# Gate and up projections of a feed-forward stage by seven block products instead of eight

## The chip, the core and the metric

The kernel runs on one core of a Trainium2 chip. The core has a matrix engine (TensorE, PE in the profile; its weight loads are listed as PEld), a vector engine (VectorE, DVE), a scalar engine (ScalarE, ACT), a general engine (GpSimd, POOL) and a queue that issues transfers (SyncE, SP). Matrix products are accumulated in eight banks of PSUM, each 2 KB for each of 128 partitions; DVE and ACT read them from there. All other operands lie in SBUF. The metric is the device time of one execution in microseconds (us).

## The reference

Two layers of a transformer-like trunk over 512 tokens of width 1024, all in float32: three token mixers merged by gates, an output projection, a feed-forward stage, and a gated input embedding. The change concerns the feed-forward stage (`D_FF` is 2816) and touches the output projection ahead of it:

```python
merged = (ga * (ya @ w_br_a[i]) + gb * (yb @ w_br_b[i])
          + gc * (yc @ w_br_c[i]))
x = x + merged @ w_o[i]
h = rmsnorm(x, norm_ffn[i])
x = x + (jax.nn.silu(h @ w_ffn_gate[i]) * (h @ w_ffn_up[i])) @ w_ffn_down[i]
h = rmsnorm(x, norm_ple[i])
x = x + jax.nn.sigmoid(h @ w_ple_gate[i]) * (p[i] @ w_ple_in[i])
```

where `rmsnorm(x, g)` is `x / sqrt(mean(x * x) + eps) * g` over the width.

## The kernel before

Activations lie transposed: a tile has 128 channels on the partitions and the 512 tokens along the free dimension, so `x` is eight tiles of 128x512. Weights are stored on the host in blocks: a block holds all input channels for 128 output channels, as 128 partitions x (k, 128).

**Products in three terms.** To keep float32 accuracy with the faster 32-bit matmul type (float32r), each operand is split into a rounded high half and the rest (`split`, L160 to L162: ACT copies the high half, L141, and DVE subtracts it from the source, L155). A product is three matmuls: high weight by high activation (L175), high by low (L176), low by high (L177). `gemm` (L179) makes one output block of 128x512 from up to eight k-blocks for each load of weights, 8 x 3 = 24 matmuls. Every matmul has its own weight load.

**Weights.** `weights` (L164) takes a raw buffer (tag `wr`), issues one transfer into it on SP's queue (L169), and splits it into `wh` and `wl`. Each of these three tags has three buffers of 128x1024. These instructions get a priority 400 places ahead of their place in the program, so that they run as early as the buffers allow.

**Order.** The order of TensorE's instructions is the order of the program (it is kept by hand). The order on the other engines is made by a scheduler at build time from the priorities and from when operands and buffers are free; on the chip each engine then works through its queue strictly in that order. Buffers of one tag are handed out as earlier tiles of the tag are released. A count of matmul groups (`chunk`, `tick`) paces side work such as the norms, which are generators that go on after so many ticks.

**The norm.** The scale of a token, `1 / sqrt(...)`, isn't known when the products of the norm's output begin. So the projections run on `x * g`, and the scale, spread over the partitions (`self.rb`), is multiplied in afterwards; what needs it is put off by `ready` until it is there. `sumsq` squares on ACT and adds up on DVE; `norm` turns the sums with PE, takes the power on POOL and turns the result back.

**Output projection, `w_o` (L859).** For each of eight blocks m: 24 matmuls, the sum with the old `x` on DVE, then `norm_chunk`: the two halves of `x * g` as a tile `h` and the square.

**Feed-forward, `ffn` (L881).** For each of two halves: 11 blocks f, each with one gate and one up product over the eight `h` (both 128x512, in banks of tag `mm`), the gate's scale, Silu, scale, product with up, and a split into `md`; then eight down blocks over the 11 `md` of this half, each added to `x` straight from its bank. The very first gate and up blocks go through `pair` (L192), which runs two output blocks over all but the last k, then the last k of both, so that the last `h` can be late. In the second half each finished `x` goes through `norm_chunk` for the next norm.

**Banks.** Eight: three of tag `mm`, two `sc`, two `tr`, one `av`. The feed-forward stage uses `mm`, and `tr` for turning the norm's sums.

A part that has matmuls of 256 columns already is `values` (L555 and on): two outputs of 128x256 share one bank, and each matmul there (L571, L573, L575) has its own weight load too.

Of the kernel before, what the change touches and what calls it, by code (L numbers as in the profile page):

```python
# [12 lines left out]
F32R = mybir.dt.float32r  # L13
I32 = mybir.dt.int32
AF = mybir.ActivationFunctionType
ALU = mybir.AluOpType
# [4 lines left out]
P = 128  # L21
L = 2
# [3 lines left out]
D = 1024  # L26
# [13 lines left out]
HB = NFB // 2  # L40
# [19 lines left out]
class Net:  # L60
# [228 lines left out]
    def build(self):  # L289
        nc, tc, a = self.nc, self.tc, self.a  # L290
        self.bufs = dict(wr=3, wh=3, wl=3, h=8, qk=2, kh=2, v=4, pt=2, y=5, z=5, x=4, t=7, rp=4,
# [15 lines left out]
    def opening(self):  # L307
# [10 lines left out]
        for _ in range(WARM):  # L318
# [5 lines left out]
                "rp": [self.sb("rp", [P, 384]) for _ in range(4)],  # L324
# [86 lines left out]
    def layer(self, i, h, xsrc, xs):  # L411
# [43 lines left out]
        h = self.ffn(h, x)  # L455
        return self.ple(h, x, xs, self.inputs())
# [302 lines left out]
    def diff_in(self, head, st, ys):  # L759
# [99 lines left out]
    def w_o(self, mg, xsrc):  # L859
        self.phase = "wo"  # L860
        xs, h, st = [], [], []
        for m in range(KD):
# [16 lines left out]
        return xs, h  # L879

    def ffn(self, h, x):  # L881
        self.phase = "ffn"
        i = self.i
        st, hn = [], []
        for half in range(2):
            mids = []
            for f in range(HB):
                fb = half * HB + f
                g = self.sb("t", [P, 512])
                md = self.sb((["z"] * 5 + ["y"] * 5 + ["pt"])[f], [P, 2, 512], F32R)  # L890
                mids.append(md)
                pg, pu = self.ps("mm"), self.ps("mm")
                if fb == 0:
                    self.pair((pg, pu), (self.a["w_fg"][i, fb], self.a["w_fu"][i, fb]), h)
                else:
                    self.gemm(pg, self.a["w_fg"][i, fb], h)

                def gate(pg=pg, g=g):
                    self.tt(g, pg, self.rb, ALU.mult)
                    self.act(g, g, AF.Silu, table="silu")  # L900
                    self.tt(g, g, self.rb, ALU.mult)

                self.ready(gate)
                if fb:
                    self.gemm(pu, self.a["w_fu"][i, fb], h)

                def up(pu=pu, g=g, md=md):
                    self.tt(g, g, pu, ALU.mult)
                    self.split(md[:, 0, :], md[:, 1, :], g)

                self.ready(up)
            for m in range(KD):
                ps = self.ps("mm")
                self.gemm(ps, self.a["w_fd"][i, half, m], mids)
                self.tt(x[m], x[m], ps, ALU.add)
                if half:
# [257 lines left out]
def _layout(v):  # L1174
# [4 lines left out]
    for i in range(L):  # L1179
# [6 lines left out]
    down = f["w_ffn_down"].reshape(L, 2, HB * P, D)  # L1186
# [14 lines left out]
        "w_fg": _blocks(f["w_ffn_gate"]),  # L1201
        "w_fu": _blocks(f["w_ffn_up"]),
        "w_fd": _blocks(down),
# [18 lines left out]
```

## Time and profile before

| | |
|---|---|
| median of 3 runs | 1824.58 us |
| lowest, highest | 1824.06, 1826.75 us |
| span of the profiled execution (no other time of it is given) | 1827.5 us |
| first layer: matmuls of gate and up, first half | 506.7 to 627.15 us |
| first layer: down blocks of the first half | 627.4 to about 687 us |
| second layer: first matmul of gate and up to the last down blocks | from about 1440 to 1768 us |
| 512 KB blocks of weights in the feed-forward stages | 44 gate, 44 up, 32 down (and 32 of 192 KB) |
| transfers issued by POOL | none |

The span is cut into 40 slices in the page's second part, a digit for the busy tenths of each. An engine's busy time alone says little for PE, since its matmuls overlap and their ends are modelled: for PE the distance between the starts of successive matmuls is what can be read. For the other engines, a row that names an idle time before it and a releaser says what the instruction waited for.

### The profile page before, as it was taken

Reading aid. Unit: us, or ns where it says so; the run is one execution under the profiler, and the core shown is the slowest. Engines: PE = TensorE matmul, PEld = TensorE weight load, DVE = VectorE, ACT = ScalarE, POOL = GpSimd, SP = SyncE. Lnnn points to the kernel's source line nnn. Section 1 sums busy time; section 2 is a strip of 40 time slices with the busy share of each in tenths; the row PEclk is TensorE's granted clock in tenths of the full one; section 3 lists DMA queues with packets and bytes.
Section 4 is the critical chain, followed back from the end, with each engine's and each line's share of the span. In section 5 each row is a group of like instructions: output and inputs, shape, how many; then the busy total and the mean of one; then the engine's idle time right before and its main releaser. Section 6 shows DMA issues by size and latency. Waiting matters only on the chain.

```text
span 1827.5 us, 23665 instructions
## 1 busy us (share of the span) xinstructions
PE 1815.3 (99%) x8820; PEld 1527.3 (84%) x8820; DVE 1191.9 (65%) x1928; ACT 763.5 (42%) x1325; POOL 24.4 (1%) x58
## 2 busy tenths in 40 slices
PE   9999999999999999999999999999999999999998
PEld 7888888888888888888888888888888888888887
DVE  7788887887654434445777878878885444344456
ACT  5476555225432222323545755452353322232334
POOL 0000000000000000000000000000000000000000
PEclk9999999999999999999999999999999999999999
DMA  5565541325423233223436655323263232322232
GB/s 199 154 195 168 147 130 45 110 96 163 151 93 103 77 110 104 93 77 108 167 121 189 188 158 153 99 70 96 97 209 106 93 104 77 116 95 93 84 112 93
DMA packets 90881, 221.13 MB, mean 121 GB/s; under 512 B 12176, under 2 KB 21776, under 8 KB 90768
## 3 DMA queue, kind: packets, MB, share of 16 engines
q1 hardware_dynamic: 89616, 218.09, 38.2%
q8 instruction: 70, 1.15, 0.3%
q10 hardware_dynamic: 1152, 1.55, 0.3%
q14 instruction: 43, 0.35, 0.1%
HBM read 180.79 MB, written 7.34 MB: 103 GB/s over the span
## 4 chain that ended last, share of the span: by engine, by line
PE 96%; DVE 2%; ACT 1%; issue 1%; DMA 0%; SPq 0%; DVEq 0%; POOLq 0%; ACTq 0%
PE ffn_mm L175 13%; PE ffn_mm L177 13%; PE ffn_mm L176 13%; PE mergea_mm L175 2%; PE mergea_mm L177 2%; PE mergea_mm L176 2%; PE diff_sc L757 2%; PE gatec_mm L175 2%; PE gatec_mm L176 2%; PE gatec_mm L177 2%; PE gateb_mm L176 2%; PE gateb_mm L175 2%; PE gateb_mm L177 2%; PE wo_mm L176 2%; PE wo_mm L175 2%; PE wo_mm L177 2%
## 5 line engine op out<-in xcount | busy, mean ns | idle before, releaser
L141 ACT ACTIVATE ffn_wh<-ffn_wr 128x1024 fp32r<-128x1024 f32 (+1 forms) x152 | 144.3, 951 | 513.3 <-issue 382.8
L175 PE MATMUL ffn_mm<-wo_h,ffn_wh 128*128 128x512 f32 x704 | 274.2, 390 | 0.0
L177 PE MATMUL ffn_mm<-wo_h,ffn_wl 128*128 128x512 f32 x704 | 273.9, 389 | 0.0
L176 PE MATMUL ffn_mm<-wo_h,ffn_wh 128*128 128x512 f32 x704 | 273.9, 389 | 0.0
L155 DVE TENSOR_TENSOR ffn_wl<-ffn_wr,ffn_wh 128x1024 fp32r<-128x1024 f32 (+1 forms) x152 | 164.8, 1085 | 130.4 <-ACT ffn_wh L141 130.4
L158 DVE SCALAR_TENSOR_TENSOR conv_z<-glu_z,pre_par,conv_z 128x512 f32<-128x512 f32 x240 | 179.3, 747 | 2.9
L177 PEld LDWEIGHTS ffn_mm<-wo_h,ffn_wl 128*128 128x128 f32 x704 | 132.2, 188 | 27.5
L176 PEld LDWEIGHTS ffn_mm<-wo_h,ffn_wh 128*128 128x128 f32 x704 | 132.2, 188 | 27.3
L175 PEld LDWEIGHTS ffn_mm<-wo_h,ffn_wh 128*128 128x128 f32 x704 | 132.2, 188 | 27.3
L155 DVE TENSOR_TENSOR ffn_t<-ffn_t,ffn_mm 128x512 f32<-128x512 f32 x44 | 30.3, 688 | 114.8 <-PE ffn_mm L177 114.7
L155 DVE TENSOR_TENSOR ffn_t<-ffn_mm,wo_r 128x512 f32<-128x512 f32 x44 | 30.4, 692 | 109.7 <-PE ffn_mm L177 109.7
L141 ACT ACTIVATE mergea_wh<-mergea_wr 128x1024 fp32r<-128x1024 f32 (+1 forms) x32 | 27.1, 848 | 96.8 <-PE mergea_mm L176 70.8
L175 PE MATMUL ffn_mm<-ffn_z,ffn_wh 128*128 128x512 f32 x160 | 62.2, 389 | 0.0
L176 PE MATMUL ffn_mm<-ffn_z,ffn_wh 128*128 128x512 f32 x160 | 62.2, 389 | 0.0
L177 PE MATMUL ffn_mm<-ffn_z,ffn_wl 128*128 128x512 f32 x160 | 62.2, 389 | 0.0
L175 PE MATMUL ffn_mm<-ffn_y,ffn_wh 128*128 128x512 f32 x160 | 62.2, 389 | 0.0
L176 PE MATMUL ffn_mm<-ffn_y,ffn_wh 128*128 128x512 f32 x160 | 62.2, 389 | 0.0
L177 PE MATMUL ffn_mm<-ffn_y,ffn_wl 128*128 128x512 f32 x160 | 62.2, 389 | 0.0
L141 ACT ACTIVATE diff_a<-diff_sc,diff_s 128x512 f32<-128x512 f32 x32 | 22.0, 687 | 60.6 <-DVE diff_s L848 60.6
L848 DVE TENSOR_REDUCE diff_s<-diff_sc 128x1 f32<-128x512 f32 x64 | 42.0, 684 | 3.1 <-PE diff_sc L757 3.0
L155 DVE TENSOR_TENSOR wo_x<-wo_x,ffn_mm 128x512 f32<-128x512 f32 x32 | 22.0, 688 | 31.4 <-PE ffn_mm L177 31.4
L141 ACT ACTIVATE natten_wh<-natten_wr 128x1024 fp32r<-128x1024 f32 x24 | 25.4, 1059 | 39.7 <-issue 17.7
(608 smaller groups left out, 4644.3 us busy)
## 6 DMA issues: line engine op xcount, KB each, us to landing
ffn_wr<-w_fg SPq DMA_DIRECT2D x44, 512.0 KB, 3.2
ffn_wr<-w_fu SPq DMA_DIRECT2D x44, 512.0 KB, 3.3
ffn_wr<-w_fd SPq DMA_DIRECT2D x32, 512.0 KB, 3.5
natten_wr<-w_in SPq DMA_DIRECT2D x16, 512.0 KB, 4.2
natten_b<-bias SPq DMA_DIRECT2D x32, 256.0 KB, 2.9
diff_wr<-w_in SPq DMA_DIRECT2D x16, 512.0 KB, 3.5
gatec_wr<-w_in SPq DMA_DIRECT2D x16, 512.0 KB, 3.7
gateb_wr<-w_in SPq DMA_DIRECT2D x16, 512.0 KB, 3.5
```

What stands on the lines that cost most here:

```text
L141: i = self.nc.scalar.activation(out, in_, func, **kw)
L155: return self.nc.vector.tensor_tensor(out, a, b, op)
L158: return self.nc.vector.scalar_tensor_tensor(out, a, s, b, op0, op1)
L175: mm(out, wh, ah, start=first, stop=False)
L176: mm(out, wh, al, start=False, stop=False)
L177: mm(out, wl, ah, start=False, stop=last)
L757: self.nc.tensor.matmul(out, st4[:, u, qs], st[:, ks], start=n == 0, stop=n == 1)
L848: nc.vector.tensor_reduce(out=m[:, u:u + 1], in_=sc, op=ALU.max, axis=AX.X, negate=True)
```

## The change

The gate and up products of two neighbouring output blocks are computed as a 2x2 block product with seven multiplications instead of eight (the Strassen form in Winograd's variant, with shared sums). The 2x2 blocks are: two output blocks of 128 channels, two halves of the input channels (even and odd k-blocks), two halves of the tokens (0 to 255 and 256 to 511). Gate and up are carried side by side in the two halves of a bank.

- `w_o` no longer makes `h`. Instead, after each even block, `halves_in` scales the two token halves and forms one difference; after each odd block, `halves_out` forms the other three sums and splits the seven 128x256 operands into high and low (a split of four blocks and one of three).
- `gate_up(step)` makes two output blocks: `seven` loads and sums the weights, `product` runs 4 k-pairs x 2 (gate, up) x 3 matmuls of 128x256. Banks x (`sc`), y (`tr`) and z (`av`) hold sums that go on: x takes products 0, 2, 4 and 6 one after the other, z products 3 and 5, and the partial sums are read out between them (`c11`, `c12`, `c22`, `c21`).
- Of the four weight sums two (`s2`, `s4`) are made by DVE; the other two (`w[1,0] + w[1,1]` and `w[1,0] + w[0,0]`) by a second transfer, issued by POOL, that adds to what the first one brought. The `wr`, `wh` and `wl` tags keep three buffers; `rp` now has two of 128x1024.
- `mid` forms `silu(gate * scale) * up`; the second scale moves behind the down product, where each down block is multiplied by it before it is added to `x`.
- The down projection is done in three parts after 4, 8 and 11 steps (8, 8 and 6 blocks), each begun by a `pair`. `pair` now leaves the last two k to the end in place of one, everywhere.
- The tiles of `p` (`pairs`) are loaded once in a layer in place of twice.

```diff
@@ pair
-        ws = [self.weights(ap, 1024) for ap in aps]
         n = len(acts)
-        for ks in (range(n - 1), (n - 1,)):
+        ws = [self.weights(ap, n * P) for ap in aps]
+        for ks in (range(n - 2), range(n - 2, n)):
@@ layer
-        h = self.ffn(h, x)
-        return self.ple(h, x, xs, self.inputs())
+        h = self.ffn(h, x, pairs)
+        return self.ple(h, x, xs, pairs)
@@ diff_in
-            raw, rot = self.sb("rp", [P, 512]), self.sb("rp", [P, 512])
+            raw, rot = self.parts_of("rp", [512], 2)
@@ w_o
-            h.append(self.norm_chunk(m, xo, self.par(self.i, "ffn", m), "h", st))
+            if m == KD - 1:
+                self.sumsq(m, xo, st)
+            if m % 2 == 0:
+                ts[m // 2] = self.halves_in(m // 2, xo)
+            else:
+                self.halves_out(ts[m // 2], xo)
+            if m < KD - 1:
+                self.sumsq(m, xo, st)
+    def halves_in(self, kp, x):
...
+        self.act(raw[0], x[:, 0:256], AF.Copy, scale=g)
+        self.act(other, x[:, 256:], AF.Copy, scale=g)
+        self.tt(raw[3], raw[0], other, ALU.subtract)
+    def halves_out(self, t, x):
...
+        self.act(raw[1], x[:, 0:256], AF.Copy, scale=g)
+        self.act(raw[6], x[:, 256:], AF.Copy, scale=g)
+        self.stt(raw[2], raw[3], -1.0, raw[6], ALU.mult, ALU.subtract)
+        self.tt(raw[4], raw[6], t["other"], ALU.subtract)
+        self.stt(raw[5], raw[2], -1.0, raw[1], ALU.mult, ALU.subtract)
+        for (h, a, z), (l, _, _), b in zip(t["hi"], t["lo"], t["bases"]):
+            self.split(h, l, b[:, 0:z - a])
+    def seven(self, step):
+        nc, w = self.nc, self.a["w_gu"][self.i, step]
+        def load(src, plus=None):
+            r = self.sb("wr", [P, 1024])
+            nc.sync.dma_start(r, src)
+            if plus is not None:
+                nc.gpsimd.dma_start(r, plus, accum_op=ALU.add)
+            return r
+        def add(a, b):
+            r = self.sb("rp", [P, 1024])
+            self.tt(r, a, b, ALU.add)
+            return r
...
+        with self.tc.high_priority(offset=min(self.w_ahead, self.tc.cur_priority - self.p0)):
+            s1 = load(w[1, 0], w[1, 1])
+            a11 = load(w[0, 0])
+            s2 = add(s1, a11)
+            o11 = parted(a11)
+            a12 = load(w[0, 1])
+            s4 = add(s2, a12)
+            o12 = parted(a12)
+            if step:
+                o2, o1 = parted(s2), parted(s1)
+            else:
+                o1, o2 = parted(s1), parted(s2)
+            return [o11, o12, o2, o1, parted(load(w[1, 0], w[0, 0])), parted(s4),
+                    parted(load(w[1, 1]))]
+    def product(self, bank, op, ts, j, kps, first):
+        mm = self.nc.tensor.matmul
+        hi, lo = op
+        for kp in kps:
+            th, tl = ts[kp][j]
+            for u in range(2):
+                begin = first and kp == 0 and u == 0
+                for n, (w, t) in enumerate(((hi, th), (hi, tl), (lo, th))):
+                    mm(bank[:, u], w[:, u, kp], t, start=begin and n == 0, stop=False,
+                       skip_group_check=True)
+            self.chunk()
+    def gate_up(self, step, ts):
...
+        x, y, z = [self.ps(tag, (P, 2, 256)) for tag in ("sc", "tr", "av")]
...
+        if step == 0:
+            for bank, n, j in ((x, 0, 0), (y, 1, 1), (z, 3, 3)):
+                run(bank, n, j, range(KP - 1), True)
+        end = range(KP - 1, KP) if step == 0 else range(KP)
+        run(x, 0, 0, end, step > 0)
+        self.act(c11, x, AF.Copy)
+        run(y, 1, 1, end, step > 0)
+        self.tt(c11, c11, y, ALU.add)
+        if step == 0:
+            run(z, 3, 3, end)
+        run(x, 2, 2)
+        self.act(c12, x, AF.Copy)
+        if step:
+            run(z, 3, 3, first=True)
+        self.act(c22, z, AF.Copy, scale=-1.0)
+        run(x, 4, 4)
+        self.tt(c22, c22, x, ALU.subtract)
+        run(z, 5, 6)
+        self.tt(c12, c12, z, ALU.add)
+        first = self.mid(2 * step, g[0])
+        run(x, 6, 5)
+        self.act(c21, x, AF.Copy, scale=-1.0)
+        return [first, self.mid(2 * step + 1, g[1])]
+    def mid(self, f, g):
...
+            self.tt(gate, gate, self.rb, ALU.mult)
+            self.act(gate, gate, AF.Silu, table="silu")
+            self.tt(gate, gate, up, ALU.mult)
+            self.split(md[:, 0, :], md[:, 1, :], gate)
@@ ffn
+        for p, (first, end) in enumerate(PARTS):
             mids = []
+            for n in range(first, end):
+                mids += self.gate_up(n, ts)
+            both = [self.ps("mm") for _ in range(2)]
+            self.pair(both, self.a[f"w_fd{p}"][i, 0:2], mids)
+            for m in range(KD):
+                if m < 2:
+                    ps = both[m]
                 else:
+                    ps = self.ps("mm")
+                    self.gemm(ps, self.a[f"w_fd{p}"][i, m], mids)
+                d = self.sb("t", [P, 512])
+                self.tt(d, ps, self.rb, ALU.mult)
+                self.tt(x[m], x[m], d, ALU.add)
```

`PARTS` is `((0, 4), (4, 8), (8, 11))` and `KP` is 4. On the host the gate and up weights are laid out by step, output block, input half and k-pair, with gate and up side by side.

More of the change, by code (lines that the diff above doesn't have):

```diff
@@ L39 @@
 NFB = DFF // P
-HB = NFB // 2
+STEPS = NFB // 2
+PARTS = ((0, 4), (4, 8), (8, 11))
+KP = KD // 2
 EPS = 1e-6
@@ L884, in ffn @@
         st, hn = [], []
-        for half in range(2):
+        for p, (first, end) in enumerate(PARTS):
             mids = []
[L887 to L894, printed above, removed]
-                else:
[L896 to L916, printed above, removed]
+            for n in range(first, end):
[5 more added lines that the diff above has]
+                    ps = both[m]
+                else:
+                    ps = self.ps("mm")
[3 more added lines that the diff above has]
+                self.tt(x[m], x[m], d, ALU.add)
+                if p == len(PARTS) - 1:
                     if m in (0, 2):
```

53 lines of the change are left out of this document (44 added, 9 removed).

## The prediction

> **What bounds the kernel now.** I read the page first, then windows and the timeline of the first layer's gate and up stretch, then the waits of SP's queue. Columns of a group: count, busy us, mean ns of one, idle time before it; columns of the timeline: start us, duration us, engine, line, operation.
>
> ```profile
> span 1827.5 us, 23665 instructions
> PE 1815.3 (99%) x8820; PEld 1527.3 (84%) x8820; DVE 1191.9 (65%) x1928; ACT 763.5 (42%) x1325; POOL 24.4 (1%) x58
> PE   9999999999999999999999999999999999999998
> DVE  7788887887654434445777878878885444344456
> PEclk9999999999999999999999999999999999999999
> PE 96%; DVE 2%; ACT 1%; issue 1%; DMA 0%; SPq 0%; DVEq 0%; POOLq 0%; ACTq 0%
> L175 PE MATMUL ffn_mm<-wo_h,ffn_wh 128*128 128x512 f32 x704 | 274.2, 390 | 0.0
> 540.00:600.00 60.00, 60.00 (x267) 49.69 (x266) 27.68 (x33) 17.43 (x22) 0.00 (x0) 1.00 0.29 98
> ```
>
> PE is never idle in the stretch of the change, its clock is granted in full (1.00), and 96% of the chain that ends last is PE. In the 60 us window the columns after the length are PE, weight loads, DVE, ACT, POOL, clock, DMA share and GB/s: DVE is busy 46%, ACT 29%, the transfers 29%. So only the number and the pitch of matmuls counts, as long as DVE, ACT and the weights keep up.
>
> The 390 ns of a matmul overlap with the next one's; what sets the end is the pitch from start to start.
>
> ```profile
> 620.57 0.39 PE L175 MATMUL ffn_mm<-wo_h,ffn_wh 128*128 128x512 f32 x1
> 626.01 0.39 PE L175 MATMUL ffn_mm<-wo_h,ffn_wh 128*128 128x512 f32 x1
> ...
> 160.20 0.28 PE L571 MATMUL diff_mm<-diff_wh,glu_h 128*128 128x256 f32 x1
> 162.96 0.28 PE L575 MATMUL diff_mm<-diff_wh,glu_h 128*128 128x256 f32 x1
> 157.22 0.28 PE L571 MATMUL diff_mm<-diff_wh,glu_h 128*128 128x256 f32 x1
> 159.60 0.28 PE L575 MATMUL diff_mm<-diff_wh,glu_h 128*128 128x256 f32 x1
> ```
>
> Between the first two rows lie 24 matmuls, one 128x512 block of eight k by three: 5.44 us, 226.7 ns each. The value projections already run 128x256 with a weight load ahead of each: 24 starts in 2.76 us (23 steps, 120.0 ns) and 21 in 2.38 us (20 steps, 119.0 ns). I take 119.7. Half the width thus costs 53% of the time, not 50%.
>
> **The change: the matmuls.** Before, 2 layers x 22 blocks x 2 (gate, up) x 24 = 2112 matmuls of 512 columns: 2112 x 0.2267 = 478.8 us. After, 22 steps (11 a layer), each seven products of 4 k-pairs x 2 (gate, up) x 3 = 24 matmuls of 256: 3696 x 0.1197 = 442.4 us, 20.1 us a step and 2.87 us a product. The difference is -36.4 us, with the two measured pitches as bounds -39.0 to -35.3. An eighth of 478.8 would be 59.9; the worse pitch takes 23.5 of it back. The Trainium skill (TensorE: Matmul & The Clock Gate, Back-to-back issue gap) gives N / 2.4 + 2.5 ns for a single warm matmul, that is 215.8 and 109.2 ns here, by which the term would be an estimate of -52 us. [...]
>
> The down projection has the same 1056 matmuls of 512 in three parts as in two; its weights come in 24 loads a layer in place of 32. Nothing on PE.
>
> **DVE and ACT per step.** Durations:
>
> ```profile
> 572.99 1.06 ACT L141 ACTIVATE ffn_wh<-ffn_wr 128x1024 fp32r<-128x1024 f32 x1 [3.85 <-issue]
> 573.96 0.62 ACT L141 ACTIVATE ffn_y<-ffn_t 128x512 fp32r<-128x512 f32 x1
> 574.09 1.23 DVE L155 TENSOR_TENSOR ffn_wl<-ffn_wr,ffn_wh 128x1024 fp32r<-128x1024 f32 x1 [0.23 <-ACT ffn_wh L141]
> 575.23 0.68 DVE L155 TENSOR_TENSOR ffn_y<-ffn_t,ffn_y 128x512 fp32r<-128x512 f32 x1
> 578.61 0.69 DVE L155 TENSOR_TENSOR ffn_t<-ffn_mm,wo_r 128x512 f32<-128x512 f32 x1 [2.69 <-PE ffn_mm L177]
> ```
>
> DVE: seven low halves and two weight sums (s2, s4) at 1.23, three bank reads and six operations of the two mids at 0.69: 11.1 + 6.2 = 17.3 us of 20.1, 86% against 46% now. ACT: seven high halves at 1.06, four bank copies and four operations of the mids at 0.62: 12.4 us, 62%. Neither is the bound by its sum. By deadlines: three buffers of each weight half let the split of operand j start when product j-3 ends, 5.74 us ahead of its use, and it needs 1.06 + 0.23 + 1.23 = 2.5 us, so 3.2 us of delay are covered (today 8.4). A bank that is read and then added to again (x after products 0, 2 and 4, z after 3) has one other product, 2.87 us, between; the read needs 0.2 + 0.69:
>
> ```profile
> 627.14 0.39 PE L177 MATMUL ffn_mm<-wo_h,ffn_wl 128*128 128x512 f32 x1
> 627.57 0.69 DVE L155 TENSOR_TENSOR ffn_t<-ffn_t,ffn_mm 128x512 f32<-128x512 f32 x1 [3.36 <-PE ffn_mm L177]
> ```
>
> (0.43 us from the last matmul's start to the reader, 0.2 past its slot.) So 2 us are spare, which one 1.23 operation ahead of it in DVE's queue fits and two don't. Queued behind a late reader is PE itself. Bounds per step: 0 if every read and split falls in its window, 1.0 if one bank read a step stands behind two wide operations (0.2 + 2 x 1.23 + 0.69 = 3.4, 0.5 over) and one split slips by as much. I take 0.2, near the lower end because the windows are longer than the work that falls into most of them: 22 x 0.2 = +4.4 (0 to +22).
>
> Where a window is missing: in step 0 of a layer product 3 has run already, so x is copied to c12 and added to by product 4 at once. PE waits 0.2 + 0.62 + some 0.1 = 0.9, at most a 1.06 copy more. Two layers: +2.0 (+1.8 to +4).
>
> **Weights.** One step reads seven blocks of 512 KB in place of 4: 3.5 MB in 20.1 us is 174 GB/s against 98; by the window's 29% at 98 that is some 52% of the DMA engines, more for the two accumulating transfers, which also read the destination. How slots and transfers follow each other now:
>
> ```profile
> SPq L169 <- DVE ffn_wl L155: 668.9, 152, 10.3
> 563.21 1.23 DVE L155 TENSOR_TENSOR ffn_wl<-ffn_wr,ffn_wh 128x1024 fp32r<-128x1024 f32 x1 [0.23 <-ACT ffn_wh L141]
> 564.46 0.33 SPq L169 DMA_DIRECT2D ffn_wr<-w_fu  x1
> DMA to landing us min/median/max: 2.2/3.2/4.8
> ```
>
> SP waits for the low half that frees one of three raw buffers and issues at once. A step now puts five raw tiles through these three: s1 (two transfers), a11, a12, the sum w10 + w00 (two) and w11. The two sums first load, then POOL waits for that landing and issues the accumulating transfer; queued behind it on POOL is only the next such transfer and one power operation per norm. The trace has no accumulating transfer and none from POOL. Its time A is bounded by a plain one (3.2 median) and twice the slowest (9.6); I take twice the median, 6.4, for two reads. The Trainium skill (Collectives: The Full Stack, Why ReduceScatter is half of AllGather) says that an add in a transfer reads two sources and so doubles the read traffic; no run here shows it, and by it A would be at most this 6.4.
>
> With time 0 at a step's start: a11's buffer is free at -3.1 (its split starts when product 4 before ends, at -5.7), w10 lands at 0.3, the sum at 0.3 + 6.4 = 6.7, its split takes until 9.3, product 4 starts at 11.5: covered. s1 is split after product 0, free at 5.5; the next s1 lands at 8.8, its sum at 15.2, s2 is added by 16.5, just before a11's buffer is wanted again at 17.0. So A = 6.4 fits, with about half a microsecond there and, once that slips, 3.5 us more at the next sum. Cost 0 in the forecast.
>
> **Ends of stages.** Into step 0 of a layer: the last x now passes a bank add, a square, two scalings, the sums and a split of four blocks.
>
> ```profile
> 506.92 0.69 DVE L155 TENSOR_TENSOR wo_x<-wo_x,wo_mm 128x512 f32<-128x512 f32 x1 [2.03 <-PE wo_mm L177]
> 507.83 1.23 DVE L155 TENSOR_TENSOR ffn_wl<-ffn_wr,ffn_wh 128x1024 fp32r<-128x1024 f32 x1 [0.23 <-ACT ffn_wh L141]
> 508.98 0.68 DVE L155 TENSOR_TENSOR wo_ss<-wo_ss,wo_t 128x512 f32<-128x512 f32 x1
> L141 ACT ACTIVATE diff_v<-diff_mm x16: 369/386/407, 170.1 to 1130.8; 128x256 fp32r<-128x256 f32 x16
> L155 DVE TENSOR_TENSOR diff_v<-diff_mm,diff_v x16: 403/415/420, 171.0 to 1131.3; 128x256 fp32r<-128x256 f32 x16
> ```
>
> 0.2 + 0.69 + 0.62 + 2 x 0.39 + 0.42 + 1.06 + 1.23 and 0.1 for each hand-over come to 5.5 us; cover is 3 products x 18 matmuls x 0.1197 = 6.5. One foreign 1.23 split in the queue makes it late by 0.2, three by 2.7. +0.5 a layer: +1 (0 to +5). In w_o each pair of blocks costs DVE about 9.1 us (two splits of 1.23, a 1024 and a 768 wide low half, four 0.69, four 0.42) in 10.9: PE hides it. At each part's end the last mid takes 0.62 + 0.69 + 0.62 + 0.69 + 0.62 + 0.69 plus hand-overs, some 4.5 us, against 36 x 0.2267 = 8.2 us of cover in the first two parts (six k, two blocks) and 24 x 0.2267 = 5.4 in the third: +0.5 a layer for the third, +1 (0 to +5). The extra multiply by the norm in every down block, 0.69 on DVE per 5.4 us, is hidden by the next block; the second load of p falls away off the path. In the other stages pair now leaves two k to the end: 8.8 us until the last k is wanted in place of 9.5, against about 4 us of work: nothing.
>
> **Sum.** -36.4 + 4.4 + 2 + 1 + 1 = -28.0 us. The profiled execution's span of 1827.5 lies 2.9 above the median of 1824.6 and is the only time that it has; 1799.5 in its terms, 1796.6 against the median. Own range: 1787 (-39 + 1.8) to 1806.
>
> **Rivals.**
> *Reads and splits slip on DVE.* DVE nearly doubles its load in the stretch (46 to 86%) and is one queue: a sum that waits for its transfer holds back the bank reads behind it. For it: only 2 us are spare per read. Against: today's queue shows gaps of 2.7 us and no waiting PE. At 0.7 us a step in place of 0.2 the time is 1796.6 + 22 x 0.5 = 1808; it takes 1.3 + 0.2 = 1.5 a step to eat the gain.
> *The accumulated sums come late (slower).* Past A = 6.9 the s2 addition delays a11's buffer, that the next w10 + w00, which holds two transfers in series; from about A = 8.3 product 4 waits, and each further microsecond of A counts twice a step, once for each sum. At 8.9 the gain is gone (1.3 x 22 = 28); at A = 9.6 it is 2.6 x 22 = 57 us, 1854. For it: three buffers for five tiles, and no row of such a transfer. Against: the transfers are busy 29% now.
> *The matmuls don't get the 256 pitch,* because four-block products change bank halves every third matmul: at 130 ns 3696 take 480 us and nothing is won, 1827 with the stalls hidden. Against: the value rows change outputs as often.
>
> **Chances.** Forecast 0.50 (1787 to 1806), slipping DVE 0.20 (1806 to 1821), unchanged within 0.2% (3.6 us, about what can be told apart here) 0.05, slower 0.25, nearly all by late sums. Faster 0.70, same 0.05, slower 0.25. The range for 8 in 10 reaches from 1787 into the late sums as far as 1835.
>
> **What would show it.** Right: 24 starts of a product in 2.76 us; PE without gaps at the bank reads except one of 0.9 us per layer ahead of product 4 in step 0; DVE at 80 to 86% and ACT near 60% in the stretch; A between 3 and 8 us; a step of 20 to 20.5 us. Wrong: PE waiting once a step for the split of the fourth or fifth operand with DVE or ACT idle (late sums), or for a bank read with DVE busy all through (slipping), or a pitch above 0.125.

## The result and the profile after

| | before | after |
|---|---|---|
| median of 4 runs each, on one chip | 1824.76 us | 1899.43 us |
| lowest, highest | 1824.06, 1826.75 us | 1896.13, 1902.25 us |
| span of the profiled execution | 1827.5 us | 1894.4 us |

The ratio is 1.0409 with an interval of 1.0393 to 1.0424: 4% slower, where 1796.6 us had been forecast (1787 to 1806, and in 8 of 10 cases up to 1835). The time lies above every case of the prediction; the farthest, late sums at A = 9.6, was 1854. The changed kernel's page:

```profile
span 1894.4 us, 27376 instructions
PE 1811.3 (96%) x10404; PEld 1598.1 (84%) x10404; DVE 1377.2 (73%) x2136; ACT 887.7 (47%) x1491; POOL 64.1 (3%) x102
PE   9999999999998998989999999999998899889998
PEclk9999999999999988999999999999999999989999
PE 73%; DMA 13%; DVE 7%; ACT 3%; issue 3%; SPq 0%; DVEq 0%; POOLq 0%; ACTq 0%
L157 DVE TENSOR_TENSOR ffn_rp<-ffn_wr,ffn_wr 128x1024 f32<-128x1024 f32 x22 | 26.9, 1225 | 94.4 <-DMA ffn_wr<-w_gu 94.4
ffn_wr<-w_gu SPq DMA_DIRECT2D x110, 512.0 KB, 3.6
ffn_wr<-w_gu POOLq DMA_DIRECT2D x44, 512.0 KB, 6.5
```

PE's busy time has fallen by 4 us only and its share of the chain that ends last from 96% to 73%; transfers, which were 0% of that chain, are 13%. The row of the 22 additions `s2` shows where: 27 us of work on DVE with 94 us of idle time before it, all of it for a transfer. The last two rows are the weights: 3.6 us (median) from issue to landing for a plain transfer on SP's queue, 6.5 for an adding one on POOL's. And the clock row, all nines before, now has eights where the feed-forward stages are.

PE's longest waits in sum (us in total, times, longest):

```profile
PE ffn_sc L975 <- DVE ffn_pt L157: 21.3, 8, 4.7
PE ffn_sc L975 <- ACT ffn_y L143: 20.9, 9, 5.7
PE ffn_sc L975 <- DVE ffn_y L157: 16.5, 6, 3.2
PE ffn_sc L975 <- ACT ffn_pt L143: 9.7, 8, 2.0
```

All four are the same kind of wait. `pt` and `y` hold the 2x2 result blocks, so PE stands before a product that adds to bank x (tag `sc`) until DVE or ACT has read that bank out. None of the four names an operand (`wh`, `wl`).

**One step.** Here is the chain of waits through one step of the first layer (start us, us, what). The step's first matmul starts at 648.10 us; the 23 and 48 matmuls are PE's work on either side of the chain.

```profile
648.27 2.77 PE ffn_sc L975 x23
...
652.15 1.24 DVE ffn_wl L157
...
653.40 3.46 DMA ffn_wr<-w_gu
...
657.53 6.80 DMA ffn_wr<-w_gu
...
664.35 0.06 DVE ffn_rp L157
...
665.50 1.22 DVE ffn_wl L157
666.72 0.61 DVE ffn_pt L157
...
667.37 7.51 PE ffn_sc L975 x48
```

The low half of `s1` frees a raw buffer at 653.4; SP loads the next `s1` into it (3.46 us) and POOL adds the second block (6.80 us); then come on DVE the addition `s2`, a low half, and only then the bank read `c22`, for which product 7 waits. DVE's and PE's rows of the timeline, with the idle time before each instruction in brackets, show that this is an order and not a dependence:

```profile
662.50 0.40 PE L975 MATMUL ffn_av<-wo_h,ffn_wh 128*128 128x256 f32 x2
...
664.35 1.23 DVE L157 TENSOR_TENSOR ffn_rp<-ffn_wr,ffn_wr 128x1024 f32<-128x1024 f32 x1 [5.22 <-DMA ffn_wr<-w_gu]
665.50 1.22 DVE L157 TENSOR_TENSOR ffn_wl<-ffn_wr,ffn_wh 128x1024 fp32r<-128x1024 f32 x1
666.63 0.68 DVE L157 TENSOR_TENSOR ffn_pt<-ffn_pt,ffn_sc 128x512 f32<-128x512 f32 x1
667.37 0.68 PE L975 MATMUL ffn_sc<-wo_h,ffn_wh 128*128 128x256 f32 x2 [1.83 <-DVE ffn_pt L157]
```

PE goes over to bank z (`av`) at 662.50, so x is complete then and `c22` could be read at 662.7. DVE was idle at that moment: it had been waiting since 659.1 for the next step's `s2`, which the build had put ahead of `c22`, and its queue is strictly in order. `c22` ran 3.9 us later than it could have.

**The clock after a wait.** The same place in three successive stretches of 3.41 us (window, length, busy us and instructions of PE, PEld, DVE, ACT, POOL, granted clock, DMA share, GB/s):

```profile
664.11:667.52 3.41, 1.58 (x13) 1.38 (x13) 3.17 (x4) 0.00 (x0) 0.00 (x0) 1.00 0.00 0
667.52:670.93 3.41, 3.41 (x17) 3.41 (x18) 2.05 (x3) 0.52 (x1) 0.00 (x0) 0.50 0.74 241
670.93:674.35 3.42, 3.42 (x30) 3.42 (x30) 3.42 (x4) 2.56 (x4) 0.72 (x1) 1.00 0.38 97
```

After the wait PE is granted half its clock for one such stretch: 17 matmuls in 3.41 us, where 28 fit at 0.1197. The stall thus costs a second time.

**The whole bill.** For the matmuls of the seven products I took the distance of each start from the start before it: what exceeds the full pitch (119.7 ns, 226.7 behind a 512 wide one) by more than 0.18 us counts as a wait, smaller excesses of over 45 ns as half clock. Two waits of 0.9 us at the end of the feed-forward stages, where PE turns the next norm's sums, are counted with the waits of every kernel that has the change.

| profiled execution | span | waits | half clock | span without both |
|---|---|---|---|---|
| before | 1827.5 us | - | - | - |
| after | 1894.4 | 79.7 | 26.7 | 1788.0 |

So the span is 39.5 us shorter without the two (36.4 forecast), and they put 106.4 back: +66.9, which is 1894.4 - 1827.5. Not all of the 39.5 is the change: the profiled execution of the kernel before waits 2.8 us for transfers in the first attention (0.6 in the changed kernel's) and has half clock from 78.5 to 85.4 us, where PE is busy 5.97 us; that is some 5 us, an estimate from these numbers. By place, of the 79.7 us 40.0 stand in front of product 7 (14 waits for `c22`) and 23.9 in front of the second product on x (11 waits for `c11`), steps 0 left out.

### The profile page after: what moved, and what is told of

Read it like the earlier page. It is cut to its first block, busy times and chain, and to the rows that moved or that the text cites. A ratio compares the mean times of both kernels' runs of the same rounds, so it can differ in the third digit from the quotient of the medians.

```text
span 1894.4 us, 27376 instructions
## 1 busy us (share of the span) xinstructions
PE 1811.3 (96%) x10404; PEld 1598.1 (84%) x10404; DVE 1377.2 (73%) x2136; ACT 887.7 (47%) x1491; POOL 64.1 (3%) x102
## 4 chain that ended last, share of the span: by engine, by line
PE 73%; DMA 13%; DVE 7%; ACT 3%; issue 3%; SPq 0%; DVEq 0%; POOLq 0%; ACTq 0%
DMA ffn_wr<-w_gu 12%; PE ffn_sc L975 7%; PE ffn_mm L177 4%; PE ffn_mm L178 4%; PE ffn_mm L179 4%; DVE ffn_wl L157 3%; PE ffn_av L975 2%; PE mergea_mm L177 2%; PE mergea_mm L179 2%; PE mergea_mm L178 2%; PE gateb_mm L178 2%; PE gateb_mm L177 2%; PE gateb_mm L179 2%; PE diff_sc L759 1%; PE gatec_mm L178 1%
## 5 line engine op out<-in xcount | busy, mean ns | idle before, releaser
L975 PE MATMUL ffn_sc<-wo_h,ffn_wh 128*128 128x256 f32 x704 | 147.4, 308 | 68.4 <-DVE ffn_pt L157 21.3
L975 PEld LDWEIGHTS ffn_sc<-wo_h,ffn_wh 128*128 128x128 f32 x704 | 120.4, 210 | 75.8 <-ACT ffn_y L143 23.0
L975 PE MATMUL ffn_sc<-wo_h,ffn_wl 128*128 128x256 f32 x352 | 106.4, 302 | 0.0
L157 DVE TENSOR_TENSOR ffn_rp<-ffn_wr,ffn_wr 128x1024 f32<-128x1024 f32 x22 | 26.9, 1225 | 94.4 <-DMA ffn_wr<-w_gu 94.4
L177 PE MATMUL ffn_mm<-ffn_z,ffn_wh 128*128 128x512 f32 x240 | 93.4, 389 | 0.0
L178 PE MATMUL ffn_mm<-ffn_z,ffn_wh 128*128 128x512 f32 x240 | 93.4, 389 | 0.0
L975 PEld LDWEIGHTS ffn_sc<-wo_h,ffn_wl 128*128 128x128 f32 x352 | 74.5, 212 | 0.0
L975 PE MATMUL ffn_sc<-wo_qk,ffn_wh 128*128 128x256 f32 x352 | 73.1, 301 | 0.0
L975 PE MATMUL ffn_sc<-wo_v,ffn_wh 128*128 128x256 f32 x352 | 70.7, 293 | 1.1 <-DVE wo_v L157 1.1
L975 PE MATMUL ffn_av<-wo_h,ffn_wh 128*128 128x256 f32 x352 | 65.3, 283 | 0.0
L975 PEld LDWEIGHTS ffn_sc<-wo_qk,ffn_wh 128*128 128x128 f32 x352 | 60.9, 212 | 0.0
L975 PEld LDWEIGHTS ffn_sc<-wo_v,ffn_wh 128*128 128x128 f32 x352 | 58.2, 203 | 1.5 <-DVE wo_v L157 1.5
```

Source lines behind the costliest of these rows:

```text
L157: return self.nc.vector.tensor_tensor(out, a, b, op)
L177: mm(out, wh, ah, start=first, stop=False)
L178: mm(out, wh, al, start=False, stop=False)
L975: mm(bank[:, u], w[:, u, kp], t, start=begin and n == 0, stop=False, skip_group_check=True)
```

## The experiments

Theory 1: the loss is waiting. Bank reads stand in DVE's and ACT's queues behind operations that wait for an adding transfer. Theory 2: the sums themselves come late, because a load and an adding transfer follow one another in too few buffers. Further rivals: the rest of the change (three down parts, the second norm scale), or the work of the adding transfers wherever it stands. All times are medians in us, ratios are against the kernel before on the same chip (1824.8 to 1827.4 us there). Waits, half clock and span are those of the profiled execution.

| kernel | time | ratio, interval | waits + half clock | span without both |
|---|---|---|---|---|
| after | 1899.43 | 1.0409 (1.0393 to 1.0424) | 79.7 + 26.7 | 1788.0 |
| eight products, rest of the change | 1827.35 | 1.0009 (1.0000 to 1.0019) | - | - |
| no second transfer | 1812.63, one run | - | 18.8 + 2.7 | 1789.3 |
| second transfer overwrites | 1846.48, one run | - | 40.5 + 12.0 | 1792.1 |
| all sums on DVE | 1851.85, one run | - | 44.5 + 13.5 | 1792.0 |
| s2, s4 behind the bank reads | 1855.7 | 1.0163 (1.0146 to 1.0181) | 50.2 + 12.5 | 1789.5 |
| and fifth operand behind c12 | 1845.78 | 1.0101 (1.0074 to 1.0127) | 41.3 + 13.0 | 1789.3 |
| filling matmuls | 1923.3 | 1.0531 (1.0515 to 1.0548) | 67.0 + 23.6 | 1829.5 |
| sums in advance, back to back | 1980.45 | 1.0855 (1.0837 to 1.0873) | 18.8 + 2.7 | 1949.0 |
| the same and both orders | 1971.83 | 1.0804 (1.0788 to 1.0821) | 16.8 + 1.7 | 1952.5 |
| sums in advance, paced | 1843.08 | 1.0101 (1.0076 to 1.0126) | 19.1 + 5.8 | 1814.9 |
| sums in late stages | 1824.48 | 0.9992 (0.9976 to 1.0008) | 20.0 + 6.1 | 1797.9 |
| the same and both orders | 1822.75 | 0.9974 (0.9963 to 0.9985) | 16.5 + 2.0 | 1793.4 |

**The rest of the change alone.**

```diff
-                mids += self.gate_up(n, ts)
+                mids += [self.plain(2 * n + u, ts) for u in range(2)]
```

`plain` is the block of the kernel before (gate and up by 512 columns over `h`), and `w_o` makes `h` again; three down parts, the late scale and the new `pair` stay.

> Gate and up as eight products in blocks of 512 as before the change, with all the rest of it: second scale behind down, down in three parts, pair with two k left, p loaded once. Every theory: within 5 us of before, 1820 to 1830 us. If it is 10 us or more slower, part of the loss is not in the seven products.

1827.35 us, +1.7, as expected: what surrounds the products costs next to nothing. Its trace has one thing that the kernel before lacks, two waits of 1.0 us ahead of the turn of the next norm's sums. The loss is inside the seven products.

**Without the second transfer.**

```diff
             nc.sync.dma_start(r, src)
-            if plus is not None:
-                nc.gpsimd.dma_start(r, plus, accum_op=ALU.add)
```

The two sums are left out: each of these operands is its first block alone.

> The second, adding transfer is left out, so that s1 and the fifth operand hold one block instead of a sum of two; VectorE, ScalarE and TensorE do all that they did. Theories 1 and 2 both: steps at 20.1 to 20.5 us, 1790 to 1802 us, the rest of the difference to 1899 being the lateness of the sums. Rival 3 (VectorE's load): still above 1850 us.

1812.63 us, 10 above the range that both theories gave and far from the third expectation (above 1850, DVE too full): 87 of the changed kernel's 1899 come with the second transfers, and DVE has the same work here. The chain through a step of the first layer:

```profile
658.12 2.88 PE ffn_tr L973 x24
...
672.52 5.76 PE ffn_sc L973 x48
678.28 2.88 PE ffn_tr L973 x24
```

Between the first and the last of these rows there is nothing but PE, its products one behind the other; from one product on y (`tr`) to the next, one step, 678.28 - 658.12 = 20.16 us, with 2.88 a product. That is the step as forecast (20.1 and 2.87). The time still lies 16 us above the forecast, and the chain at the start of a layer shows what is left:

```profile
511.93 1.24 DVE ffn_wl L157
...
513.20 0.60 ACT ffn_wh L143
513.79 0.49 ACT ffn_pt L143
...
514.33 3.02 PE ffn_sc L973 x23
```

In step 0 the second product on bank x waits for the copy `c11`, behind three high halves on ACT. The distances of starts give 2.13 us there, 1.61 at the next product on x and 0.33 later, in each layer, and 2.2 at two later steps of each, where `c11` stands behind a weight's and a `mid`'s high half.

**Order on DVE.** `s2` and `s4` of the next step may not come ahead of the bank reads `c22` and `c12` of the step before in DVE's queue; nothing else is changed.

```diff
-            s2 = add(s1, a11)
+            s2 = add(s1, a11, self.c22 if step else None)
...
-            s4 = add(s2, a12)
+            s4 = add(s2, a12, self.c12 if step else None)
```

> Order alone is changed: the two weight sums on VectorE (s2, s4 of the next step) may not be queued ahead of the bank reads c22 and c12 of the step before. Theory 1 (the queue's order: s2 waits for the accumulating transfer until 16.2 us into a step, and the bank read that was ready at 14.6 and the split of w11 stand behind it): the waits of TensorE for c22 before the seventh product go, and with them its half-speed stretches; a step falls from 23.7 to 26 us to 20.1 to 21, the time to 1795 to 1815 us. Theory 2 (the accumulated sum itself is late for three raw buffers): the wait only moves from the bank read to a later operand, steps stay at 23 us or more, 1865 us or more. Rival 3 (VectorE at 86% is too full whatever its order): 1850 us or more, with VectorE busy without gaps.

1855.7 us: 44 us won, by order alone, so the order is a cause; but the time lies between what the two theories gave. It lies in the range of the third expectation, that DVE is too full, but that one wanted DVE busy without gaps: DVE still idles 39.5 us ahead of the 22 `s2`, and the kernel without the second transfer does the same work on DVE in 1812.63. The waits ahead of product 7 (40.0 us) are gone; those ahead of the second product on x rise from 23.9 to 32.6. PE now waits for ACT's copies, not for DVE:

```profile
PE ffn_sc L984 <- ACT ffn_y L144: 26.2, 7, 6.6
PE ffn_sc L984 <- ACT ffn_pt L144: 13.9, 12, 2.0
```

The chain of one such wait:

```profile
698.12 8.58 DMA ffn_wr<-w_gu
...
706.72 0.95 DVE ffn_rp L158
...
707.87 1.23 DVE ffn_wl L158
...
709.11 3.51 DMA ffn_wr<-w_gu
...
713.29 5.78 DMA ffn_wr<-w_gu
...
719.15 1.06 ACT ffn_wh L144
720.21 1.01 ACT ffn_y L144 x2
...
721.27 0.80 PE ffn_sc L984 x2
```

This is theory 2's chain: the adding transfer for `s1` took 8.58 us, `s2` and the low half of a11 follow, only then is a raw buffer free for `w10 + w00`, which loads (3.51) and adds (5.78); its high half stands in ACT's queue ahead of the copy of bank x, `c11`, and PE waits 6.4 us for that copy.

**Order on ACT too.** As above, with the high half of the fifth operand (`w10 + w00`) behind the copy `c12`.

```diff
-            self.split(hi, lo, raw)
+            self.behind(self.act(hi, raw, AF.Copy), after)
+            self.tt(lo, raw, hi.bitcast(F32), ALU.subtract)
...
-        self.act(c12, x, AF.Copy)
+        ops += rest(self.act(c12, x, AF.Copy))
```

> As e1_reads_first, and on ScalarE the high half of the fifth operand (the sum w10 + w00) may not be queued ahead of the copy of bank x to c12 in its own step. Theory 1, now for both queues (a split that waits for an adding transfer holds back a bank copy that was ready): the 40 us in which TensorE waited for ScalarE's copies in e1 fall to under 15, the half-speed stretches behind them go, 1800 to 1825 us. Theory 2 (the sums are late whatever the order): the waits come back at the fifth product as waits for the split, 1845 us or more.

1845.78 us, another 10, at the edge of theory 2's range: 54.3 us of waits and half clock remain, so the two orders were worth 52 of the 106.4. The waits didn't fall to under 15 us, as theory 1 had it, nor did they move to the fifth product, as theory 2 had it: PE waits 20.5 us for copies on ACT and 12.0 us for a half of an operand, more than half of this within a step's first product. That what is left is mostly late sums is shown only by the kernels below that move the transfers.

**What in the second transfer costs.** It overwrites the first block in place of adding to it (the operand is then the second block alone):

```diff
-                nc.gpsimd.dma_start(r, plus, accum_op=ALU.add)
+                nc.gpsimd.dma_start(r, plus)
```

> The kernel of e3_plain_second once more, whose matmuls all ran at 0.555 of the clock. The second transfer landed in 3.7 us there against 6.5 when it adds. With the clock granted in full: landing 3.5 to 4.5 us and 1805 to 1825 us, near e2_no_second_transfer, if the adding is what makes the sums late; near 1899 if GpSimd's issuing is.

1846.48 us. (An earlier run of the same code, expected at 1795 to 1820 us or within 10 of 1899, ran at 0.555 of the clock from end to end and took 2963.8 us, which says nothing of either.) A plain second transfer from POOL takes 4.5 us in the median and costs 34 us over none; the adding (6.5) costs another 53, each from single runs. So both the second place in the chain and the length of the transfer count; the landing is as the first expectation had it, the time as neither.

Then the four sums all on DVE, the second block through a raw buffer of its own:

```diff
-                nc.gpsimd.dma_start(r, plus, accum_op=ALU.add)
+                q = self.sb("wr", [P, 1024])
+                nc.sync.dma_start(q, plus)
+                self.tt(r, r, q, ALU.add)
```

> The adding transfers are replaced by a plain load of the second block into a raw buffer of its own and a sum on VectorE: 11 wide operations a step in place of 9, 19.8 us of VectorE's time in 20.1. Theory 1: no queue waits for an adding transfer any more; what is left is VectorE's load at 98%, 1815 to 1850 us. If VectorE's load was the cause all along, 1900 us or more.

1851.85 us, just above theory 1's 1815 to 1850: seven raw tiles through three buffers, and PE waits for ACT (30 us) and for splits.

**Filling the wait.** Sixteen matmuls of zeros (256 columns) into a spare bank ahead of product 7 of each step, to keep the clock up.

```diff
+        spare = self.ps("mm", (P, 2, P))
+        for _ in range(16):
+            self.nc.tensor.matmul(spare, self.zero_r, self.zero_r[:, None, :].to_broadcast([P, 2, P]),
+                                  start=True, stop=True)
         run(x, 6, 5)
```

> The changed kernel with its own queues, and 16 matmuls of zeros (128x256, 1.9 us, into a bank that nobody reads) ahead of the seventh product of each step, where TensorE waits 2 to 5 us for the bank read. If the idle time is what halves the matmul rate behind it (0.213 in place of 0.120 us a matmul for 18 to 30 matmuls, 1.7 to 2.8 us a step), the filled wait keeps the rate up and the time falls by 20 to 45 us, to 1855 to 1880. If the half rate has another cause, the fill brings nothing or adds up to 42 us: 1895 to 1940.

1923.3 us, in the second range, though not for the cause that it names. The filling adds 42 us of work (22 x 16 x 0.12; the span without waits and half clock rises from 1788.0 to 1829.5) and takes back 12.7 of the waits and 3.1 of the half clock. The waits ahead of product 7 fall from 40.0 to 3.8 us, but those ahead of the next step's second product on x rise from 23.9 to 49.2: PE now waits for the copies on ACT and gets half the clock after those waits. The adding transfers come no sooner (7.1 us in the median), so the wait has only moved.

**The sums made in advance.** Outside the feed-forward stages POOL copies one block into a scratch in DRAM and adds the other there; a step reads the sum with one plain transfer. Full output.

```diff
+            self.nc.gpsimd.dma_start(self.sums[key], self.a["w_gu"][i, n, 1, 0])
...
+            self.nc.gpsimd.dma_start(self.sums[self.half], src, accum_op=ALU.add,
+                                       max_dma_last_dim=2048)
...
-            s1 = load(w[1, 0], w[1, 1])
+            s1 = load(self.sums[self.i, step, 1])
```

> The two weight sums that came by an adding transfer just ahead of their use are made in advance: outside the feed-forward stages POOL copies one block of a sum into a scratch in DRAM and a turn later adds the other block to it there; a step then reads each sum with one plain transfer on SP's queue. Everything else as in the changed kernel, the output is the full one. Theory 1 (the loss is the second transfer standing between a load and what waits for it, on the way to a split and in front of other work in DVE's and ACT's queues): the time falls to that of the kernel without the second transfer, 1805 to 1820 us, under the kernel before. Theory 2 (what costs is the adding transfers' work itself, 44 of 512 KB through the same DMA engines, wherever it stands, or the other stages' loads now collide with it): at most half of the 87 us comes back, 1850 us or more.

> As the kernel with the sums made in advance, with both orders on top: the sums of the next step stand behind the bank reads c22 and c12 in DVE's queue, the high half of the fifth operand behind the copy c12 in ACT's. Theory 1a (with plain transfers nothing in front of the bank reads waits any more): no difference to the kernel with the sums in advance, within 4 us, PE keeps the waits of step 0 and of the last mid of a part. Theory 1b (some of the bank reads still stand behind work that waits): another 8 to 15 us fall, 1797 to 1806 us.

1980.45 and 1971.83 us, far above theory 1 and by their time in theory 2's range. But the feed-forward stages did what theory 1 says: 21.5 us of waits and half clock, to a tenth the figures of the kernel without the second transfer, 18.5 with the orders. It is the rest of the kernel that lost 160 us. PE's longest waits of the first of the two:

```profile
PE natten_tr L705 <- POOL natten_e L687: 111.6, 10, 46.2
PE glu_tr L246 <- POOL glu_rc L242: 15.8, 1, 15.8
```

Nothing held the copies back, so the 44 sums followed one another in POOL's queue (1.3 to 319 us, 7.2 us each), each addition waiting for its copy, and the small memory sets that POOL does for the first attention stood among and behind them. It is the changed kernel's fault once more, on another engine.

Paced: each copy waits for a matmul of its own layer, one sum every 18 groups of three matmuls, from the second attention on.

> As the kernel with the sums in advance, whose 44 sums POOL issued back to back from the first microsecond to 319 us, ahead of its own work for the first attention (PE waited 112 us for POOL there), while its feed-forward stages kept only 21.5 us of waits. Here each copy waits for a matmul of its own layer, one sum every 18 groups of three matmuls (about 12 us), from the second attention to the output projection, when POOL's work for the first attention is over. Full output. Theory 1 (the loss of the change is where the adding transfers stand): 1805 to 1818 us, under the kernel before. Theory 2 (the adding transfers cost other stages what they save, wherever they go): 1830 us or more.

1843.08 us, in the range of theory 2, but its reason isn't borne out: the feed-forward stages keep 24.9 us in place of 106.4, 81.5 saved, and the span without both rises by 26.9. Its windows show where most of that is lost, and where not:

```profile
140.00:190.00 50.00, 45.86 (x276) 39.93 (x275) 35.72 (x82) 29.86 (x73) 3.61 (x8) 0.97 0.75 189
190.00:240.00 50.00, 46.12 (x271) 39.90 (x270) 39.72 (x71) 23.46 (x50) 3.38 (x6) 1.00 0.73 183
...
340.00:410.00 70.00, 70.00 (x310) 57.95 (x310) 63.09 (x86) 20.66 (x29) 8.05 (x12) 1.00 0.70 175
410.00:470.00 60.00, 60.00 (x269) 49.30 (x268) 45.44 (x72) 30.31 (x51) 8.02 (x11) 1.00 0.83 235
```

Between 140 and 240 us, where the attentions move small tiles about, PE is busy 92 of 100 us (99 in the kernel before; from 1050 to 1150 us, in the second layer, it is 91 against 99); from 340 on it is busy all through with the DMA engines nearly as full or fuller. So the last pair makes the sums from the gates of the third branch to the output projection, one every 16 groups, and the last few in the first part's down projections:

```diff
-AHEAD = ("diff", "gatec", "gateb", "branchc", "mergea", "pin", "mergeb", "wo")
+AHEAD = ("gateb", "branchc", "mergea", "pin", "mergeb", "wo")
...
-        if self.phase in AHEAD:
+        if self.phase in AHEAD or self.down:
             self.presum()
```

> As the paced kernel, but the sums are made elsewhere: in the paced one PE lost its time between 140 and 290 us (the two attentions, whose small transfers between buffers then came late) and none from 290 us on, where the sums ran as well. Here one sum is made every 16 groups from the gates of the third branch to the output projection, and the last few in the down projections of the first part. Full output. Theory 1 (the loss of the change is only where the adding transfers stand): 1808 to 1818 us, with 19 to 25 us of waits and half-rate matmuls left in the feed-forward stages. Theory 2 (the sums cost the other stages as much as they save, wherever they are made): 1824 us or more.

> As the kernel with the sums in the late stages, with both orders on top (the sums of the next step behind the bank reads in DVE's queue, the high half of the fifth operand behind the copy c12 in ACT's). The two kernels with the sums made back to back kept 21.5 and 18.5 us of waits in the feed-forward stages, so 3 us less are expected: 1805 to 1815 us. If a transfer still held back a queue it would be 8 us or more.

1824.48 us, no difference to the kernel before, and 1822.75 with both orders, a ratio of 0.9974 (0.9963 to 0.9985): the seven products with 44 adding transfers of the same size, 77 us under the changed kernel and a little under the kernel before. Both lie above what theory 1 gave (1808 to 1818 and 1805 to 1815), and the first reaches theory 2's "1824 us or more" by half a microsecond; the ten runs of the last one go from 1813.7 to 1824.3. But the sums don't cost the other stages what they save: the feed-forward stages keep 26.1 and 18.5 us of the 106.4 (19 to 25 expected for the first), and the spans without both, 1797.9 and 1793.4, lie 10 and 5 above the 1788.0. The traces show where these are lost. In the first layer PE waits 2.6 and 2.5 us for POOL's power operation in the convolution's norm, which stands in POOL's queue behind an addition that waits for its copy, and the next 3.41 us run at half clock; the kernel before has neither. The first of the two kernels also has the kernel before's waits for transfers (2.7 us) and 6.83 us of half clock in the first attention, where the changed kernel waits 0.6 us and keeps its full clock. DVE's timeline in a step of the last kernel:

```profile
566.55 0.69 DVE L183 TENSOR_TENSOR ffn_pt<-ffn_pt,ffn_sc 128x512 f32<-128x512 f32 x1 [0.74 <-PE ffn_sc L1021]
567.16 1.22 DVE L183 TENSOR_TENSOR ffn_rp<-ffn_wr,ffn_wr 128x1024 f32<-128x1024 f32 x1
568.29 1.22 DVE L183 TENSOR_TENSOR ffn_wl<-ffn_wr,ffn_wh 128x1024 fp32r<-128x1024 f32 x1
```

The order is now `c22` (waiting for PE, as it should), `s2`, a low half, and `s2` no longer waits for anything.

## Why the prediction was wrong

- **The matmul term was right.** A product takes 2.88 us (2.87 forecast) and an undisturbed step 20.16 (20.1); over 154 products that is -35.3 us, where -36.4 was forecast. The spans without waits and half clock lie 35 to 40 us under 1827.5 in six kernels (1788.0 to 1792.1), with some 5 us of the kernel before's own waits in them. The rival with the worse pitch is out.
- **The transfers came when forecast, within 1 us.** With time 0 at the start of the step shown, 648.1: `s1` landed at 8.8 (8.8 forecast), its sum at 16.2 (15.2), `s2` was done at 17.5 (16.5). A is 6.5 us in the median; 6.4 was taken.
- **The step that failed is "Cost 0 in the forecast" together with "0.2 us a step" for DVE.** Both were worked out stream by stream: operand deadlines with the transfers' times, bank reads with the lengths of DVE's operations. The forecast had `s2` wait until 15.2 and end at 16.5, and it had the bank read `c22` free to run from 14.6 (662.7 - 648.1) with one 1.23 us operation ahead of it at most. It never asked which of the two is first in DVE's queue. `s2` was, so the read inherited the transfer's lateness. In place of 4.4 us for slipping reads and 0 for the weights, the waits and half clock come to 106.4 over 22 steps, 4.8 a step, of which order alone took away 52.1 and moving the transfers alone 84.9 (the two overlap).
- **The slipping rival named the mechanism and got its price wrong.** It said that a sum that waits for its transfer holds back the bank reads behind it, and then priced that at 0.7 us a step, the length of one bank read. DVE's idle time in front of `s2` was 94.4 us, 4.3 a step: the price of an in-order queue is the wait of what stands first, not its work.
- **The late-sums rival was half right.** It was to begin beyond A = 6.9 and decide at 8.9. A was 6.5, but single transfers went to 8.58 us, and with the orders mended 54.3 us remained, of which 35.8 went when the sums were made in advance (54.3 to 18.5). It shows mostly as a copy held behind a high half on ACT, where the rival looked for product 4 waiting for its operand.
- **"PE waits 0.9 ... Two layers: +2.0" was too small.** In step 0 and just behind it the copies cost 2.13 + 1.61 + 0.33 = 4.1 us a layer, because the first is `c11`, which the forecast didn't list, behind three high halves. With the four later waits of 2.2 that is 16.9 of the 18.8 us that stay without second transfers, and the two waits at the norm's sums are the other 1.9, against 4 forecast for step 0 and all stage ends.
- **That a wait also costs clock was in no term:** 26.7 of the 106.4 us.
- **The rest held, but for one wait:** three down parts, the second scale, `pair` and `p` cost +1.7 us together. The multiply in the down blocks was to be hidden by the next block; behind the last one there is none, and there PE waits 1.0 us a layer for the norm's sums, which no run sets apart from the rest of the change.

Not settled: the medians of the last two kernels lie 6 and 8 us above what theory 1 gave. The profile of the last one, its quickest run (1813.7 us), is within it and has a mean granted clock of 0.998; its slower runs have 0.995 to 0.997. A share of 0.003 of 1820 us is 5.5, about half of the 10 us between its runs, an estimate; no trace shows the waits of the slower runs.

## What to carry to other kernels

Draw the queue of each in-order engine for one period of the loop, with the time at which each entry can start, and price an entry that waits for a transfer by its whole wait for everything behind it. An engine at 73% can be the bound without being busy. A serial pair of transfers in front of an operand belongs where its lateness meets no queue that something else needs: making the sums early won 85 us in the stage, and cost 160 elsewhere until POOL's queue was looked at in the same way.

## What the runs showed of the hardware

**The clock after short waits.** In the changed kernel's feed-forward stages the granted clock was always 1.00 or 0.50 and changed only on a grid of 3.41 us. Of the stretches of this grid at full clock, 14 were followed by one at 0.50, and each of them held 1.99 us or more of waiting; the others held 2.01 us at most, all but one 1.81 or less. A wait that lies across two stretches may go free. In the kernel with the sums in late stages the same 2.13 us wait falls in one stretch in the first layer and across two in the second:

```profile
518.69:522.10 3.41, 1.45 (x13) 1.24 (x12) 2.64 (x3) 3.41 (x5) 0.45 (x1) 1.00 0.01 2
522.10:525.51 3.41, 3.41 (x18) 3.41 (x18) 1.61 (x3) 0.19 (x1) 0.00 (x0) 0.50 0.47 154
...
1416.34:1419.75 3.41, 2.71 (x21) 2.29 (x19) 3.13 (x5) 2.06 (x3) 0.65 (x1) 1.00 0.14 55
1419.75:1423.17 3.42, 1.59 (x13) 1.59 (x14) 3.42 (x4) 2.27 (x4) 0.38 (x1) 1.00 0.19 31
1423.17:1426.58 3.41, 1.99 (x17) 1.74 (x16) 1.60 (x3) 1.94 (x3) 0.00 (x0) 1.00 0.31 125
```

The Trainium skill (TensorE: Matmul & The Clock Gate, What's actually happening) gives a free-running window of 3413 ns, and these rows agree; its advice for a kernel (Why this matters for your kernels) is to leave no gap of more than about 3 us, and here 2 us within one window were enough.

**Adding transfers.** 512 KB added to what lies in SBUF took 6.5 us in the median and 8.8 at most, against 4.5 for the same transfer from POOL without the add and 3.6 for one on SP's queue; POOL itself is busy 0.88 us with the issue. So the add made the transfer 1.4 times as long, where the forecast took 2 times the 3.2 of a plain one; the rest of A is the 4.5 that a plain one from POOL took in this place.
